# Dilated attention queries: one stored copy, laid out in rows of 128 per head by ScalarE, and projection blocks finished one at a time

## The chip, the cores and the metric

The kernel runs on one NeuronCore of a Trainium2 chip, as one program. The metric is device time in microseconds (us) of one execution, taken as the median of several. Engines are named as in the profile: PE (TensorE, matmuls), PEld (its weight loads, of the stationary operand), DVE (VectorE), ACT (ScalarE), POOL (GpSimd), SP (SyncE, which here only issues transfers). A letter q behind a name (SPq, ACTq, POOLq) is the engine's instruction queue when it issues a transfer. All matmul operands are float32 numbers, split into a rounded high part and the rest, so that one product is made of two or three matmuls.

## The reference

One decoder layer on 1024 tokens of width 1024. What matters here is the attention branch: 12 heads of 64 columns, three configurations with a softmax over each, weighted by their log-sum-exp. The kernel computes the third (dilation 16) inside the second (dilation 4): on 1024 tokens all that it reaches lies a multiple of four away, and a table of offsets counts twice what both reach. So it has two configurations, 0 and 1.

```python
C_HEADS = 12; HEAD_DIM = 64
C_CONFIGS = ((128, 1), (512, 4), (2048, 16))     # (window, dilation)

def _mixer_c(q, k, v, rel_table):
    q = q.reshape(bsz, s, C_HEADS, HEAD_DIM) * (HEAD_DIM ** -0.5)
    for window, dil in C_CONFIGS:
        o, l = _dilated_attn(q, k, v, window, dil, rel_table)   # blocks of 128 tokens, own and previous block
        outs.append(o); lses.append(l)
    wts = jax.nn.softmax(jnp.stack(lses, axis=0), axis=0)
    o = jnp.einsum('nbsh,nbshe->bshe', wts, jnp.stack(outs, axis=0))

z = xn @ w_in          # au, av, bx, bg, cq, ck, cv, z: all projections of the normed input
merged = gate_a * (out_a @ p_a) + gate_b * (out_b @ p_b) + gate_c * (out_c @ p_c)
x = x + g1 * (merged @ w_out)      # then the gated MLP, a second residual, a final norm
```

With dilation 4 a block holds every fourth token: queries 512j+r, 512j+r+4, and so on (a set r of four, j of two halves).

## The kernel before, in words

The program is one long run of matmuls on PE with all else arranged around it. It goes through these stages, in time of the profile: the norm and the first projections (0 to 192 us), the stream of projections (192 to 785 us), the attention (785 to 1190 us), the output projection, the gated MLP and the end (1190 to 1981 us).

**The stream.** A unit projects two blocks of 128 columns for all tokens in seven products (`ORDER`: A11, A12, S1, S2, S3, A22, S4), one in each slot, each of 12 matmuls. Results are evacuated into one tile `ot` (two buffers) that holds both blocks, m0 and m1. The first block m0 is complete with S4, the seventh slot, the second m1 with A22, the sixth. S3 adds into the PSUM bank that S2 has filled, so PE may start S3 only when ScalarE has evacuated S2 (line 165). S4 adds into bank z, which must first be read by line 269 on DVE, after line 267 on ACT. Behind the last slot of a unit `post` handles the two blocks: an activation over each (line 677) and a store to DRAM (678), or, for the queries and keys, `split_heads`, a generator that is put on the list `side` and of which one step is taken in each slot.

**Queries and keys.** `split_heads` makes the high part h of a block (ACT, line 924) and the low part in place (DVE, 927 or 929). For queries each of the two is also copied into an order in which the tokens of a block of 128 are sorted by their remainder r by 4 (ACT, line 933), and all four versions go to DRAM (918): sorted high and low, plain high and low. Keys are stored in two versions.

**Attention.** For a head `load_head` loads all four versions of q (1024 KB, line 1063, by POOL's queue) and k with both parts doubled (1065), and the bias table by SP's queue. `logits` (1197) makes one PSUM bank in each of seven slots. Slots 0 to 3 are configuration 0: the sorted queries `qp`, 128 columns that lie next to each other, are the stationary operand, 128 or 256 keys the moving one. Slots 4 to 6 are configuration 1: the stationary operand is `qn[:, 512*j+r : 512*j+r+509 : 4]`, the moving one `kt[:, r : r+4n-3 : 4]`, both with a step of four numbers. Slots 4 and 5 have four matmuls with 128 moving columns and then two with 256, slot 6 has four with 256. DVE adds the bias and takes the maximum (1219), ACT the exponential (1222), POOL works out the factors (`factors`, 1225), DVE scales and PE transposes (`turn`, 1249), PE multiplies with the values (`outputs`, 1265).

**Order.** In the stream the order on all five engines is written by hand (`Stream`). In the attention only PE's is: each step of a head h has a place in head units (load at h - 0.55, logits at h + 0.08 s, and so on), and between them lie steps of the `filler` (lines 1125 to 1159), the branch outputs times p_a, p_b, p_c (tile `gp`). The order on ACT, DVE, POOL and SP is set by a scheduler, so an edit in one place can shift rows in others. An engine works its queue in order: what waits holds all behind it.

**The seam** at 785 us: the last unit of the stream still runs while the first logits and the filler's first operands (`oT`, loaded by SP in line 1117 and split by ACT in line 116 and DVE or POOL in 117) come in, on the same ACT and DVE queues.

Of the kernel before, what the change touches and what calls it, by code (L numbers as in the profile page):

```python
# [36 lines left out]
LEAD, DQ, TM, DP, DO = 0.55, 0.08, 1.05, 0.11, 0.18  # L37
# [32 lines left out]
def trunk(ctx: ExitStack, tc: tile.TileContext, I: dict, out: bass.AP, dbg=None):  # L70
# [22 lines left out]
    def rows_scr(name, n):  # L93
# [3 lines left out]
    qk_scr = {n: [dram.tile(sh, F32, name=f"{n}{h}_scr") for h in range(NH)]  # L97
              for n, sh in (("q", [2, 2, HD, S]), ("k", [2, HD, S]))}
# [174 lines left out]
    def stream_ws(gb, tcomb, views, ot, post):  # L273
# [10 lines left out]
        for i, (wn, tn, bk) in enumerate(ORDER):  # L284
# [631 lines left out]
    def store_heads(name, ix, j, t):  # L916
        for i in range(2):
            nc.scalar.dma_start(qk_scr[name][2 * j + i][ix], t[HD * i:HD * i + HD, :])

    def split_heads(name, j, m, scale, hlp):  # L920

        mf = m.rearrange("p a b -> p (a b)")
        h = hlp().tile([P, S], F32R, tag="hl", bufs=3, name="hl")
        act.activation(h, mf, AF.Copy, scale=scale)
        yield
        if scale == 1.0:
            dve.tensor_tensor(mf.bitcast(F32R), mf, h.bitcast(F32), op=OP.subtract)
        else:
            dve.scalar_tensor_tensor(mf.bitcast(F32R), mf, scale, h.bitcast(F32), op0=OP.mult, op1=OP.subtract)
        for c, src in enumerate((h.bitcast(F32), mf)):  # L930
            if name == "q":
                dst = hlp().tile([P, S], F32, tag="hl", bufs=3, name="hlp")
# [5 lines left out]
            else:  # L938
                yield
# [787 lines left out]
```

## Time and profile before

| | us |
|---|---|
| median of 3 runs (lowest, highest) | 1984.4 (1983.62, 1989.04) |
| the profiled execution | 1982.27 |
| its span, first to last instruction | 1980.6 |
| PE, busy in the span | 1874.4 |
| DVE, busy in the span | 1287.9 |
| ACT, busy in the span | 899.5 |
| POOL, busy in the span | 633.8 |

The profile is read from PE: where PE has no idle time, work that other engines save costs or gives nothing, and only what PE itself issues counts. Where PE idles, the row names what ended the wait. Starts of matmuls that follow each other give the rate at which PE gets through them, which the durations in the rows don't, since matmuls overlap.

### The profile page before, as it was taken

How to read it: one execution, taken by the hardware profiler on the slowest of the kernel's cores; microseconds unless marked ns; L12 is line 12 of the kernel's file. 1: busy time of each engine (PE TensorE's matmuls, PEld its weight loads, DVE VectorE, ACT ScalarE, POOL GpSimd, SP SyncE). 2: the span in 40 equal slices, each digit the busy share in tenths (PEclk: the TensorE clock that was granted, in tenths of full speed). 3: DMA queues.
4: the chain of work that ended last, by engine and by line, in shares of the span. 5: the costliest groups of instructions: out<-in, count | busy, mean ns of one | idle time of the engine just before them, and what ended most of it. 6: DMA issues, size and time to landing. Idle time of an engine off the chain costs nothing.

```text
span 1980.6 us, 26351 instructions
## 1 busy us (share of the span) xinstructions
PE 1874.4 (95%) x9119; PEld 1508.4 (76%) x9119; DVE 1287.9 (65%) x2259; ACT 899.5 (45%) x1644; POOL 633.8 (32%) x1067
## 2 busy tenths in 40 slices
PE   6899999999999899899899999999999999999996
PEld 5767898877767677677777777877787887877885
DVE  6766576666666675555555765569767666557786
ACT  5344556664335633534434533444433443344543
POOL 6310000003111111244555565456544444300002
PEclk9899999999999999899999999999999999999998
DMA  9232435435556888777677445413334333477674
GB/s 326 70 122 84 140 104 165 140 129 173 172 178 218 291 243 235 217 167 188 166 167 186 126 169 181 150 64 123 122 114 149 99 97 124 135 271 254 201 228 147
DMA packets 248118, 328.61 MB, mean 166 GB/s; under 512 B 16551, under 2 KB 167315, under 8 KB 247984
## 3 DMA queue, kind: packets, MB, share of 16 engines
q1 hardware_dynamic: 197664, 184.07, 31.4%
q10 hardware_dynamic: 33744, 87.18, 12.1%
q0 software_dynamic: 16576, 55.67, 10.1%
q8 instruction: 72, 1.18, 0.2%
q14 instruction: 62, 0.51, 0.1%
HBM read 238.64 MB, written 88.22 MB: 165 GB/s over the span
## 4 chain that ended last, share of the span: by engine, by line
PE 72%; DMA 9%; DVE 6%; issue 6%; POOL 3%; ACT 2%; SPq 1%; ACTq 0%; DVEq 0%; POOLq 0%
PE g L191 18%; PE g L295 18%; PE gp L1152 7%; PE g L334 6%; PE g L1615 6%; PE go L1407 4%; PE sl L1214 3%; DMA adaw<-in_w_ada_dram 2%; PE g L215 2%; PE tp L1258 1%; PE o L1287 1%; PE gp L1370 1%; PE m L788 1%; DMA res<-x_scr 1%; PE o L1290 1%
## 5 line engine op out<-in xcount | busy, mean ns | idle before, releaser
L295 PE MATMUL g<-xs,wh 128*128 128x512 f32 x1344 | 435.9, 405 | 31.1 <-ACT ot L165 21.7
L191 PE MATMUL g<-xs,wh 128*128 128x512 f32 x1176 | 367.6, 394 | 9.5 <-DVE up L168 2.7
L295 PEld LDWEIGHTS g<-xs,wh 128*128 128x128 f32 x1344 | 251.3, 190 | 107.8 <-ACT ot L165 32.1
L116 ACT ACTIVATE wh<-raw 128x512 fp32r<-128x512 f32 (+2 forms) x251 | 147.2, 601 | 274.2 <-issue 58.8
L191 PEld LDWEIGHTS g<-xs,wh 128*128 128x128 f32 x1176 | 220.3, 188 | 63.0 <-ACT xs L116 3.1
L295 PE MATMUL g<-xs,wl 128*128 128x512 f32 x672 | 267.9, 399 | 0.0
L191 PE MATMUL g<-xs,wl 128*128 128x512 f32 x588 | 230.4, 393 | 0.0
L117 DVE TENSOR_TENSOR wl<-raw,wh 128x512 fp32r<-128x512 f32 (+2 forms) x180 | 129.8, 727 | 84.2 <-ACT wh L116 84.0
L1152 PE MATMUL gp<-oT,wh 128*128 128x512 f32 x512 | 171.7, 415 | 4.4 <-ACT oT L116 1.9
L295 PEld LDWEIGHTS g<-xs,wl 128*128 128x128 f32 x672 | 127.8, 190 | 31.2
L117 POOL TENSOR_TENSOR wl<-st,wh 128x512 fp32r<-128x512 f32 x63 | 104.0, 1651 | 144.3 <-ACT wh L116 139.4
L117 POOL TENSOR_TENSOR wl<-raw,wh 128x512 fp32r<-128x512 f32 (+2 forms) x71 | 92.3, 1301 | 123.1 <-ACT wh L116 108.4
L254 ACT ACTIVATE wh<-st 128x512 fp32r<-128x512 f32 x120 | 75.2, 627 | 120.6 <-DVE st L252 120.4
L191 PEld LDWEIGHTS g<-xs,wl 128*128 128x128 f32 x588 | 110.5, 188 | 24.9
L334 PE MATMUL g<-wh,xs 128*128 128x256 f32 x672 | 124.8, 286 | 0.0
L116 ACT ACTIVATE wh<-st 128x512 fp32r<-128x512 f32 x95 | 59.3, 628 | 138.9 <-PE g L191 96.8
L1222 ACT ACTIVATE pm<-pm,stat 128x128 f32<-128x128 f32 (+1 forms) x192 | 89.0, 465 | 58.0 <-DVE stat L1219 57.9
L1152 PEld LDWEIGHTS gp<-oT,wh 128*128 128x128 f32 x512 | 89.8, 192 | 27.2 <-issue 7.7
L334 PEld LDWEIGHTS g<-wh,xs 128*128 128x128 f32 x672 | 103.7, 188 | 1.6 <-issue 1.0
L1615 PE MATMUL g<-wl,wh 128*128 128x512 f32 x264 | 103.5, 392 | 0.0
L1615 PE MATMUL g<-wh,wl 128*128 128x512 f32 x264 | 103.4, 392 | 0.0
L1152 PE MATMUL gp<-oT,wl 128*128 128x512 f32 x256 | 102.7, 401 | 0.0
(321 smaller groups left out, 3790.2 us busy)
## 6 DMA issues: line engine op xcount, KB each, us to landing
raw<-in_w_in_dram SPq DMA_DIRECT2D x66, 512.0 KB, 5.7
raw<-in_f_wdown_dram SPq DMA_DIRECT2D x77, 256.0 KB, 3.7
adaw<-in_w_ada_dram SPq DMA_DIRECT2D x48, 256.0 KB, 5.4
g_scr<-ot ACTq DMA_DIRECT2D x24, 512.0 KB, 5.2
adaw<-in_w_ada_dram POOLq DMA_DIRECT2D x48, 256.0 KB, 5.1
raw<-g_scr SPq DMA_DIRECT2D x24, 512.0 KB, 3.6
qk<-q_scr POOLq DMA_DIRECT2D x12, 1024.0 KB, 6.1
qk<-k_scr POOLq DMA_DIRECT2D x24, 512.0 KB, 9.6
```

The source lines that it names most:

```text
L116: act.activation(h, src, AF.Copy)
L117: l_eng.tensor_tensor(l, src, h.bitcast(F32), op=OP.subtract)
L191: pe.matmul(banks[bk], a[:, k, :], b, start=(fresh and j == 0), stop=(j == 11), skip_group_check=True)
L215: pe.matmul(banks[i, h], a[:, k, :], b, start=(fresh and j == 0), stop=(not fresh and j == 11), skip_group_check=True)
L254: act.activation(it["h"], bl[name], AF.Copy)
L295: pe.matmul(banks[bk], a[:, k, :], b, start=(fresh and j == 0), stop=(j == 11), skip_group_check=True)
L334: pe.matmul(banks[t2][bk][:, 256 * i:256 * i + 256], a[:, sl], b[:, k % 2, :], start=(fresh and i == 0 and j == 0), stop=(j == 11), skip_g ...
L1152: pe.matmul(pt, a_[:, k % g, :], b_, start=(j == 0), stop=(j == 3 * n - 1))
L1214: pe.matmul(sb[:, of:of + n], lq, kt[:, ks], start=(of == 0 and kt is kh), stop=(kt is kl), skip_group_check=True)
L1222: act.activation(pm[:, of:of + n], pm[:, of:of + n], AF.Exp, scale=-1.0, bias=stt[:, cfg, 0, idx:idx + 1], accum_out=stt[:, cfg, 1, idx:id ...
L1407: pe.matmul(pt, a_[:, sl], b_, start=(k == 0 and j == 0), stop=(k == KD - 1 and j == 2))
L1615: pe.matmul(bank, a_[:, sl], b_, start=(start and j == 0), stop=(j == 2), skip_group_check=True)
```

## The change

Queries are stored in one version only, sorted, in two parts (high and low). The high part is written sorted in the one pass of ACT, the low part by four DVE instructions of 256 columns, and both parts of queries and keys have tiles of their own (`hl`), so that `ot` isn't written any more. `load_head` loads 512 KB of q. For configuration 1 a new step `turn_queries` copies the loaded sorted queries with two ACT instructions of 128x512 into a tile `qd`, in which the 128 queries of a set stand next to each other; slots 4 to 6 take their stationary operand from there, with a step of one. The keys keep their step of four. The load of a head moves from h - 0.55 to h - 1.2 (0.3 h for the first), `turn_queries` stands at h - 0.3, for head 0 at the end of the stream. In every unit of the stream the block m1 is finished by itself after A22, and m0 after S4.

```diff
-LEAD, DQ, TM, DP, DO = 0.55, 0.08, 1.05, 0.11, 0.18
+LEAD, DQ, TM, DP, DO = 1.2, 0.08, 1.05, 0.11, 0.18
@@ stream_ws
-                return later + (post(m0, m1) if wn == "S4" else [])
+                return later + (post(0, m0) if wn == "S4" else post(1, m1) if wn == "A22" else [])
@@ project
-        def post(m0, m1):
-            flat = [m.rearrange("p a b -> p (a b)") for m in (m0, m1)]
-            res = [(1, lambda i=i: act.activation(flat[i], flat[i], f)) for i in (1, 0) if f]
-            return res + [(2 if f else 1, lambda i=i: nc.scalar.dma_start(dst[j + i], flat[i])) for i in (1, 0)]
+        def post(i, m):
+            flat = m.rearrange("p a b -> p (a b)")
+            return [(1, lambda: act.activation(flat, flat, f)), (2, lambda: nc.scalar.dma_start(dst[j + i], flat))]
@@ split_heads
-        h = hlp().tile([P, S], F32R, tag="hl", bufs=3, name="hl")
-        act.activation(h, mf, AF.Copy, scale=scale)
+        h, l = [hlp().tile([P, S], F32R, tag="hl", bufs=3, name="hl") for _ in range(2)]
+        if name == "q":
+            by4 = [t.rearrange("p (t r i) -> p t r i", t=NT, r=4) for t in (h, l)]
+            src = mf.rearrange("p (t i r) -> p t r i", t=NT, r=4)
+            act.activation(by4[0], src, AF.Copy, scale=-0.125)
+            yield
+            for r in range(4):
+                dve.scalar_tensor_tensor(by4[1][:, :, r, :], src[:, :, r, :], -0.125, by4[0][:, :, r, :].bitcast(F32),
+                                         op0=OP.mult, op1=OP.subtract)
+        else:
+            act.activation(h, mf, AF.Copy)
+            yield
+            dve.tensor_tensor(l, mf, h.bitcast(F32), op=OP.subtract)
+        store_heads(name, 0, j, h.bitcast(F32))
         yield
-        if scale == 1.0:
-            dve.tensor_tensor(mf.bitcast(F32R), mf, h.bitcast(F32), op=OP.subtract)
-        else:
-            dve.scalar_tensor_tensor(mf.bitcast(F32R), mf, scale, h.bitcast(F32), op0=OP.mult, op1=OP.subtract)
-        for c, src in enumerate((h.bitcast(F32), mf)):
-            if name == "q":
-                dst = hlp().tile([P, S], F32, tag="hl", bufs=3, name="hlp")
-                act.activation(dst.rearrange("p (t r i) -> p t r i", t=NT, r=4),
-                               src.rearrange("p (t i r) -> p t r i", t=NT, r=4), AF.Copy)
-                store_heads("q", (1, c), j, src)
-                yield
-                store_heads("q", (0, c), j, dst)
...
+        store_heads(name, 1, j, l.bitcast(F32))
@@ load_head, and new
-        nc.gpsimd.dma_start(qq, qk_scr["q"][h].rearrange("a c b s -> (c b) a s"))
+        nc.gpsimd.dma_start(qp, qk_scr["q"][h].rearrange("c b s -> (c b) s"))
+    def turn_queries(qp):
+        qd = heads["hd"].tile([P, S], F32R, tag="qd", bufs=1, name="qd")
+        for j in range(0, S, HALF):
+            act.activation(qd[:, j:j + HALF].rearrange("p (r c i) -> p r c i", r=4, c=4),
+                           qp[:, j:j + HALF].bitcast(F32).rearrange("p (c r i) -> p r c i", r=4, c=4), AF.Copy)
+        return qd
@@ logits
-                    lq = qn[:, 512 * j + r:512 * j + r + 509:4]
+                    lq = st_["qd"][:, P * idx:P * idx + P]
@@ head_steps
-        yield h - LEAD, load
+        yield max(h - LEAD, 0.3 * h), load
+        if h:
+            yield h - 0.3, turn_heads
```

What this does to the queues is shown at three places. The first is ACT in the stream, in a unit of queries (`ot<-g` are the evacuations of lines 161, 165 and 267, `wh` the high parts of the next weights, `hl` and `hlp` the split queries, `q_scr` their store). Before, from the first slot's evacuation to line 165:

```order
L161 ACTIVATE ot<-g 128x512
L254 ACTIVATE wh<-st 128x512
L924 ACTIVATE hl<-ot 128x1024
L254 ACTIVATE wh<-raw 128x512
L933 ACTIVATE hlp<-hl 128x1024
L918 DMA q_scr<-hl 64x1024 x2
L254 ACTIVATE wh<-raw 128x512
L918 DMA q_scr<-hlp 64x1024 x2
L933 ACTIVATE hlp<-ot 128x1024
L918 DMA q_scr<-ot 64x1024 x2
L165 ACTIVATE ot<-g 128x512
```

and in the changed kernel, over the same slots:

```order
L926 ACTIVATE hl<-ot 128x1024
L161 ACTIVATE ot<-g 128x512
L254 ACTIVATE wh<-st 128x512
L917 DMA q_scr<-hl 64x1024 x2
L254 ACTIVATE wh<-raw 128x512
L917 DMA q_scr<-hl 64x1024 x2
L926 ACTIVATE hl<-ot 128x1024
L254 ACTIVATE wh<-raw 128x512
L917 DMA q_scr<-hl 64x1024 x2
L165 ACTIVATE ot<-g 128x512
```

Of the passes over 1024 columns only the 926 of block m0 stands between lines 161 and 165 now, with a weight split and two stores behind it; the copy 933 that stood directly ahead of line 165 is gone.

The second place is ACT at the seam (numbered tiles: `ot_6831` is the last unit's result, `oT_...` the filler's operands, `wh` with 128x384 the filler's weights, `pm` the first logits). Before:

```order
L165 ACTIVATE ot_6831<-g_6816 128x512
L116 ACTIVATE oT_7003<-oT_7004 128x512
L116 ACTIVATE wh_7280<-raw_7278 128x384
L116 ACTIVATE oT_6978<-oT_6979 128x512
L116 ACTIVATE wh_7284<-raw_7278 128x384
L267 ACTIVATE ot_6831<-g_6816 128x512
L1222 ACT_TABLE_LOAD
```

and in the changed kernel (`ot_6814` is the last unit's result there):

```order
L165 ACTIVATE ot_6814<-g_6799 128x512
L116 ACTIVATE oT_6987<-oT_6988 128x512
L116 ACTIVATE oT_6962<-oT_6963 128x512
L267 ACTIVATE ot_6814<-g_6799 128x512
L116 ACTIVATE wh_7283<-raw_7281 128x384
L116 ACTIVATE wh_7287<-raw_7281 128x384
L1230 ACT_TABLE_LOAD
```

Line 267 comes ahead of the two weight splits. In SP's queue the load of the `oT` that is split just ahead of line 267 also comes ahead of the load of those weights, and not behind it. Further on, ACT has `qd` of head 0 between the last unit's sigmoid and the exponentials of slot 2:

```order
L677 ACTIVATE ot_6814<-ot_6814 128x1024
L116 ACTIVATE oT_6977<-oT_6978 128x512
L116 ACTIVATE oT_7007<-oT_7008 128x512
L677 DMA g22_scr_139<-ot_6814 128x1024
L1076 ACTIVATE qd_6910<-qp_6781 128x512 x2
L1230 ACT_TABLE_LOAD
L1230 ACTIVATE pm_7058,stat_7017<-pm_7058,stat_7017 128x256 x2
L116 ACTIVATE oT_6982<-oT_6983 128x512
```

The third place is POOL in the attention, around the loads of one head (`sw`, `ex`, `dd`, `fc` are the factors, `wl` a low part of the filler's weights, `v` the values). Before:

```order
L1247 COPY fc<-ex 32x2 x16
L117 TENSOR_TENSOR wl<-raw,wh 128x384
L1171 COPY v_7695<-stat 1x1
L1175 COPY v_7698<-stat 1x1
L1230 COPY sw<-stat 32x4 x8
L1063 DMA qk<-q_scr 128x2x1024
L1065 DMA qk<-k_scr 64x2x1024 x2
```

and in the changed kernel:

```order
L1255 COPY fc<-ex 32x2 x16
L117 TENSOR_TENSOR wl<-raw,wh 128x384
L1057 DMA qp<-q_scr 128x1024
L1174 COPY v_7701<-stat 1x1
L1178 COPY v_7704<-stat 1x1
L1238 COPY sw<-stat 32x4 x8
L1059 DMA qk<-k_scr 64x2x1024 x2
```

The load of q stands earlier, ahead of the next head's first factor copies; the load of k stays where it was.

## Rows read from the trace of the kernel before

**Rows 1.** Busy us by stage: length, PE, PEld, DVE, ACT, POOL, granted clock, DMA share, GB/s.

```profile
620.00:700.00 80.00, 73.41 (x307) 56.42 (x305) 54.51 (x81) 49.64 (x53) 14.10 (x27) 0.98 0.87 286
785.00:825.00 40.00, 28.78 (x107) 21.94 (x106) 17.27 (x51) 22.64 (x53) 7.76 (x19) 0.83 0.80 240
825.00:1190.00 365.00, 357.33 (x2113) 283.35 (x2112) 213.41 (x717) 154.81 (x495) 199.95 (x574) 0.99 0.67 169
```

**Rows 2.** The same view, three stretches at the lower granted clock.

```profile
653.70:657.00 3.30, 3.15 (x7) 2.48 (x8) 1.88 (x4) 1.67 (x3) 1.03 (x2) 0.50 1.02 394
797.00:803.70 6.70, 4.71 (x11) 3.75 (x12) 3.32 (x8) 6.64 (x14) 1.07 (x1) 0.50 0.54 176
950.60:957.30 6.70, 5.00 (x18) 3.98 (x19) 4.53 (x17) 4.35 (x14) 3.13 (x3) 0.50 0.55 187
```

**Rows 3.** Timeline of PE, query units (start, length, operation, count [idle before, what ended it]).

```profile
629.67 0.72 PE L295 MATMUL g<-xs,wh 128*128 128x512 f32 x2 [0.69 <-ACT ot L165]
...
653.85 1.22 PE L295 MATMUL g<-xs,wh 128*128 128x512 f32 x2 [3.08 <-ACT ot L165]
...
679.16 0.73 PE L295 MATMUL g<-xs,wh 128*128 128x512 f32 x2 [2.81 <-ACT ot L165]
```

**Rows 4.** Timeline of ACT ahead of the second of these waits.

```profile
651.28 2.03 ACT L933 ACTIVATE hlp<-ot 128x1024 f32<-128x1024 f32 x1 [0.73 <-DVE adaa L975]
```

**Rows 5.** Timeline of PE at the seam, three of its waits.

```profile
788.47 0.73 PE L295 MATMUL g<-xs,wh 128*128 128x512 f32 x2 [2.19 <-ACT ot L165]
...
798.99 1.22 PE L295 MATMUL g<-xs,wh 128*128 128x512 f32 x2 [4.64 <-DVE ot L269]
...
812.98 0.50 PE L1152 MATMUL gp<-oT,wh 128*128 128x512 f32 x1 [0.56 <-ACT oT L116]
```

**Rows 6.** Timeline of ACT at the seam.

```profile
792.89 0.53 ACT L116 ACTIVATE wh<-raw 128x384 fp32r<-128x384 f32 x1 [3.31 <-DMA raw<-in_p_a_dram]
796.29 0.63 ACT L116 ACTIVATE oT<-oT 128x512 fp32r<-128x512 f32 x1 [2.88 <-DMA oT<-oa_scr]
...
797.24 0.58 ACT L267 ACTIVATE ot<-g 128x512 f32<-128x512 f32 x1
797.84 1.28 ACT L1222 ACT_TABLE_LOAD   x1
```

**Rows 7.** Timeline of PE, logits with a step of four, stretches of single matmuls.

```profile
1016.64 0.42 PE L1214 MATMUL sl<-qk 128*128 128x128 f32 x1
...
1016.88 0.54 PE L1214 MATMUL sl<-qk 128*128 128x256 f32 x1
...
1017.23 0.42 PE L1214 MATMUL sl<-qk 128*128 128x256 f32 x1
...
1022.67 0.42 PE L1214 MATMUL sl<-qk 128*128 128x256 f32 x1
...
1022.90 0.42 PE L1214 MATMUL sl<-qk 128*128 128x256 f32 x1
```

**Rows 8.** The same, logits with a step of one (two of 128, two of 256 columns).

```profile
1006.63 0.62 PE L1214 MATMUL sl<-qk 128*128 128x128 f32 x4
...
1006.80 0.45 PE L1214 MATMUL sl<-qk 128*128 128x256 f32 x2
...
1006.97 0.28 PE L1214 MATMUL sl<-qk 128*128 128x256 f32 x1
1007.09 0.39 PE L1152 MATMUL gp<-oT,wh 128*128 128x512 f32 x1
```

**Rows 9.** Weight loads by form, step four, then step one (count, busy us, mean ns).

```profile
L1214 PEld LDWEIGHTS sl<-qk 128*128 128x128 f32 x4 | 1.0, 328 | 0.2 <-issue 0.2
...
L1214 PEld LDWEIGHTS sl<-qk 128*128 128x128 f32 x4 | 0.5, 190 | 0.0
```

**Rows 10.** Timelines of POOL and PE around the longest wait inside the attention.

```profile
944.69 1.30 POOL L117 TENSOR_TENSOR oT<-oT 128x512 fp32r<-128x512 f32 x1 [5.11 <-ACT oT L116]
...
952.30 1.12 PE L1287 MATMUL o<-st,v 128*64 128x128 f32 x6 [4.44 <-DVE st L1263]
```

More of the change, by code (lines that the diff above doesn't have):

```diff
@@ L96, in trunk @@
     z_scr = {n: rows_scr(n, KW) for n in ("au", "bx", "bg")}
-    qk_scr = {n: [dram.tile(sh, F32, name=f"{n}{h}_scr") for h in range(NH)]
-              for n, sh in (("q", [2, 2, HD, S]), ("k", [2, HD, S]))}
+    qk_scr = {n: [dram.tile([2, HD, S], F32, name=f"{n}{h}_scr") for h in range(NH)]
+              for n in "qk"}
     g_scr = rows_scr("g", 3 * KD)
@@ L942, in project_heads @@
-    def project_heads(name, j, hlp):
-        def post(m0, m1):
-            def queue():
-                for i, m in ((1, m1), (0, m0)):
-                    side.append(split_heads(name, j + i, m, -0.125 if name == "q" else 1.0, hlp))
-            return [(1, queue)]
+        h, l = [hlp().tile([P, S], F32R, tag="hl", bufs=3, name="hl") for _ in range(2)]
[11 more added lines that the diff above has]
+            dve.tensor_tensor(l, mf, h.bitcast(F32), op=OP.subtract)
@@ L950, in project_heads, with post @@
+        store_heads(name, 0, j, h.bitcast(F32))
+        yield
+        store_heads(name, 1, j, l.bitcast(F32))
+    def project_heads(name, j, hlp):
+        def post(i, m):
+            return [(1, lambda: side.append(split_heads(name, j + i, m, hlp)))]
         return stream_ws(gb1, tcomb, pair_views(COL["c" + name], j), ot2, post)
@@ L1057, in load_head @@
     def load_head(h):
-        def tl():
-            return heads["hd"].tile([P, 2, S], F32R, tag="qk", bufs=2, name="qk") if h % 2 == 0 else \
-                wk.tile([P, 2, S], F32R, tag="ot", bufs=2, name="qk")
-        qq, kk = tl(), tl()
-        nc.gpsimd.dma_start(qq, qk_scr["q"][h].rearrange("a c b s -> (c b) a s"))
+        if h % 2 == 0:
+            qp = heads["hd"].tile([P, S], F32R, tag="qp", bufs=1, name="qp")
+            kk = heads["hd"].tile([P, 2, S], F32R, tag="qk", bufs=1, name="qk")
+        else:
+            qp, kk = [wk.tile([P, 2, S], F32R, tag="ot", bufs=2, name="qk") for _ in range(2)]
+            qp = qp[:, 0]
+        nc.gpsimd.dma_start(qp, qk_scr["q"][h].rearrange("c b s -> (c b) s"))
         for i in range(2):
             nc.gpsimd.dma_start(kk[HD * i:HD * i + HD], qk_scr["k"][h].rearrange("c b s -> b c s"))
-        qp, qn, kh, kl = qq[:, 0], qq[:, 1], kk[:, 0], kk[:, 1]
+        kh, kl = kk[:, 0], kk[:, 1]
         bt = heads["hd"].tile([P, 2, 256], F32, tag="bt", bufs=2, name="bt")
@@ L1075, in load_head @@
                 nc.sync.dma_start(bt[32 * q:32 * q + 32, cfg, :], src)
-        return qp, qn, kh, kl, bt
+        return qp, kh, kl, bt
+    def turn_queries(qp):
[4 more added lines that the diff above has]
+        return qd
     phase(["hd"], queue_heads)
@@ L1080, in trunk @@
     stream.call(marks)
+    heads["qd"] = turn_queries(heads[0][0])
     head0 = heads[0]
@@ L1191, in load, with turn_heads @@
             st_["in"] = load_head(h) if h else head0
+            if h == 0:
+                st_["qd"] = heads["qd"]
             st_["s"] = ap.tile([P, 2, 2, 8], F32, tag="stat", bufs=2, name="stat")
+        def turn_heads():
+            st_["qd"] = turn_queries(st_["in"][0])
         def values():
@@ L1197, in logits @@
         def logits(s_):
-            qp, qn, kh, kl, bt = st_["in"]
+            qp, kh, kl, bt = st_["in"]
             stt = st_["s"]
```

9 lines of the change are left out of this document (3 added, 6 removed).

## The prediction

> **What bounds the kernel now.** I read the busy time of each engine by stage first, then PE's waits inside a stage, then the starts of single matmuls. PE is the busiest engine in each of the stages that the change touches [rows 1]. So a gain must be PE idle time that goes, work that PE itself does faster, or a stretch at the lower clock that isn't entered. The stages differ. In the query units (620 to 700 us) PE idles 6.6 of 80 us, at the seam (785 to 825) 11.2 of 40, in the attention proper (825 to 1190) only 7.7 of 365 [rows 1]. In the first two a wait is the subject; in the third only what PE issues counts, as ACT (154.8 us), POOL (200.0) and DVE (213.4) have room in 365 us [rows 1]. From 1190 us on the change alters nothing but a few rows of the scheduler's order, which I cost at nothing.
>
> All sums are made against the profiled execution, 1982.3 us. It is 2.1 us below the median of 1984.4, so I take the gain off the median at the end.
>
> **Query units.** PE waits ahead of S3 for ACT's evacuation of S2: 0.69 us in the ordinary case, but 3.08 and 2.81 us in two of the three query units [rows 3]. The reader sees why in ACT's rows: the copy of line 933 runs from 651.28 for 2.03 us, line 165 can start only behind it, near 653.3, and PE goes on at 653.85 [rows 3, 4]. Each query block now has one strided pass on ACT in place of one plain and two strided ones, and none of it stands directly ahead of line 165. What is left between: block m0's pass, which I take to be as long as the strided copy, 2.03 us [rows 4], a split of weights and two store issues. A slot of 12 matmuls takes some 3.0 us (from 653.85 to 679.16 [rows 3], less the wait of 2.81 and 1.6 for the half clock below, in seven slots), and m0's pass is queued in the third slot, so it should be over before S2, in the fourth, ends. Both waits then fall to 0.69: 3.08 + 2.81 - 1.38 = 4.5 us. The first of them is also followed by 3.3 us at half clock, 1.2 GHz, with PE busy for 3.15 [rows 2]; at full clock that work takes half, 1.6 us less. Gain 6.1; if one of the waits stays, 3.
>
> The four DVE instructions replace one of the same 1024 columns. Even at twice its length DVE has cover, 54.5 of 80 us busy [rows 1], and what queues behind them are weight splits made four slots ahead. The extra function-table loads on ACT (1.28 us each [rows 6], three more by the order, where two sigmoids or gelus no longer stand together) lie in slots where line 165 isn't due; nothing for them. If a table load did fall ahead of an evacuation, it would cost its 1.28 us; this is inside the margin. Finishing m1 a slot sooner frees `ot` earlier, for which PE doesn't wait: nothing.
>
> **The seam.** PE's longest wait is 4.64 us ahead of S4, for line 269, which needs line 267 [rows 5]. ACT started 267 at 797.24 because the split ahead of it waited until 792.89 for weights and the next one until 796.29 for an `oT` load [rows 6]. S3 began at 788.47 [rows 5] and its 12 matmuls end near 791.5. In the new order neither the weights nor a late `oT` stands ahead of 267 (SP issues that `oT` load before the weights'), so 267 runs at some 791.6, DVE follows, and S4, two slots behind S3, starts without a wait near 794.5. That is 4.6 us, and up to 4.71 / 2 = 2.4 more if the half-clock stretch from 797 [rows 2] isn't entered.
>
> What is late next: the filler's operands. ACT's chain from the table load at 797.84 [rows 6] to the split that PE awaited at 812.98 [rows 5] takes 15.1 us, nearly all of it work on ACT. In the new kernel the table load comes after the two weight splits, whose data landed at 792.89, so near 793.9, 4 us sooner. Two `qd` passes are inserted, by ACT's nearest 128x512 row 0.63 each [rows 6], and a pair of exponentials and two splits move behind. So PE gets those operands some 4 us earlier, not 7. I take 4, with ends 0 (the chain eats it) and 7 (both parts of the wait's price).
>
> **The logits with dilation 4.** Here PE's own work changes, 12 heads with 16 such matmuls each, 8 of 128 and 8 of 256 moving columns. With a step of four one load takes 328 ns, with a step of one 190 [rows 9]. What counts is the spacing of starts. Step four: 1016.64 to 1016.88, 0.235 us, ahead of a 256; 1022.67 to 1022.90, 0.235 as well, for 256 columns [rows 7]. Step one: two of 128 and two of 256 take 0.46 together, 0.115 each, and the last 256 takes 0.12 [rows 8]. If only the load were slow, all 16 would gain 0.12.
>
> But the keys keep their step of four, and one row tells that they are slow too. With step four, the start that follows the first 256 comes 0.35 later, 1016.88 to 1017.23 [rows 7]; 0.235 is the load, so 0.115 is what 256 columns take beyond 128. With step one the same place has 1006.80 to 1006.97, 0.17 [rows 8], 0.05 beyond 0.115. 128 more columns cost twice as much with the step: streaming is at half rate as well, some 0.117 for 128 and 0.235 for 256. Then a 256 stays at 0.235 whatever its load does, and only the 128s gain, 8 x (0.235 - 0.117) = 0.94 us a head. The first load of a slot is 0.138 longer with the step [rows 9] and not hidden where short matmuls stand ahead, in about two slots of three: 0.2 a head. Together 1.1 x 12 = 13 us. Ends: 2 (only the first loads count) and 25 (all 16 gain 0.12, and the first loads). I take 13, since the 0.35 is measured in this very operation. The Trainium skill (SBUF — State Buffer, section "Door 1: The DMA port swizzle") says that reads which go to a new 16-byte line each time lose bandwidth; four float32 are 16 bytes, and it makes no difference between queries and keys, which speaks against the full 25. The two rows agree.
>
> **Its price on other engines.** Two ACT passes a head, 12 x 2 x 0.63 = 15 us, or twice that, of work on an engine with 210 us of room in this stage [rows 1]. In ACT's order they stand mostly ahead of slot 6's exponentials of the head before and must wait for that slot's logits on PE, 0.08 head away; the exponentials behind would wait for the same logits. The rows are due at slot 4, half a head later. Nothing. The transfers shrink from 1024 to 512 KB a head, with DMA at 0.67 [rows 1]: nothing. POOL gets the q load earlier in its queue; behind it stand factor copies and weight splits. The tile that it fills was given free at logits that PE has finished by then: nothing. The wait of 4.44 us at 952.30 comes from a split on POOL that waited 5.11 us with the factor copies behind it [rows 10]; that order hardly changes and the wait stays.
>
> **Sum.** 6 + 4 + 13 = 23 us: 1959 for the profiled execution, 1961 as a median.
>
> **Rivals.**
> 1. *The loads alone are slow.* The logits gain 25, the sum is 35: 1949 us. For it: 328 against 190 ns is plain [rows 9]. Against it: the 0.35 [rows 7]. The same time would follow if loads did not run beside matmuls at all: 192 x 0.138 = 26 us. Against that stands a spacing of 0.235 that is shorter than the load's 328 [rows 7, 9]. The Trainium skill (TensorE: Matmul & The Clock Gate, section "The mechanism") lets loads overlap running matmuls only when they use other row groups; the trace doesn't agree. Chance 0.14.
> 2. *The attention gives it back.* PE gets ahead, and the filler's operands, already late at the seam, or POOL's chain become the limit; the logits' gain shrinks to 2: 6 + 4 + 2 = 12, 1972 us. For it: the schedule is not re-timed to PE, and POOL is busy 200 of 365 us in long chains [rows 1, 10]. Against it: PE waits just 7.7 us there now. Chance 0.18.
> 3. *Slower: the earlier load of q holds POOL.* If at that place its tile isn't free, POOL stands with factor copies and weight splits behind it, as at 944.69. One such hold costs what that one does: 4.44 us of wait, and 5.00 / 2 = 2.5 of work at half clock behind it [rows 2, 10], 7 us. Three holds leave a gain of 2; from the fourth head on the kernel is slower, 1961 + 28 = 1989, at eight of twelve heads 2017. For it: one tile for `qp` and `qd` each, where q and k had two buffers. Against it: by the order the freeing logits stand more than half a head ahead. Chance 0.06.
> 4. *It does what it says, and it doesn't matter:* waits only move and the half-clock stretches come elsewhere; 1980 to 1984. Chance 0.04.
>
> **How the numbers follow.** Forecast 0.58, the rivals 0.14, 0.18, 0.06, 0.04. The range takes the ends of the three terms: 6 + 7 + 25 = 38 gives 1946, 3 + 0 + 2 = 5 gives 1979; I cut the upper end to 1977, since all three low ends at once are unlikely. This leaves out rivals 3 and 4 and part of 2. Within 0.3% (6 us, about what a measurement of this kernel can tell from no change): 0.06, rival 4 and a bit of 2. Faster 0.88, slower 0.06.
>
> **What would show it.** PE's waits ahead of S3 in the query units at 0.7 and no half clock there; no wait ahead of the last S4 and the seam shorter by about 4; in slots 4 and 5 starts 0.12 apart for 128 columns, in slot 6 still 0.235. If slot 6 runs at 0.12, rival 1 holds. If new waits for `oT`, `wl` or the factors appear in the attention, rival 2 or 3. A wait of logits for `qd` would prove the cover wrong.

## The result, and the profile after

The changed kernel takes 1956.8 us (median of 4 runs, 1955.37 to 1959.26) against 1984.9 (4 runs of the kernel before beside it): a ratio of 0.986, 95% interval 0.984 to 0.988. The forecast was 1961 with a range from 1946 to 1977; the time fell by 28 us where 23 had been forecast. The profiled execution took 1959.3, the slowest of the four; its span is 1957.6 against 1980.6, so 23.0 less, as the sum said. That it comes out to the microsecond is luck: 26.8 were gained up to the last logits, and 3.8 lost behind them. This table is read from the starts of PE's rows in the two profiles. The profiled execution of before was 2.6 us faster than the median beside it, that of the change 2.5 slower; this is why the median fell by 5 us more than the profile.

| PE starts (us) | before | after | after less before | forecast |
|---|---|---|---|---|
| first logits | 785.2 | 780.9 | -4.3 (3.8 of it in the query units) | -6 |
| first `gp` | 806.0 | 795.4 | -10.6, so -6.3 at the seam | -4 |
| last logits | 1137.5 | 1110.7 | -26.8, so -16.2 in the attention | -13 |
| end of the span | 1980.6 | 1957.6 | -23.0, so +3.8 behind it | 0 |

The busy time of PE over the whole span in the profile after (share, instructions), and then the same view of stretches as [rows 1]; the seam now lies some 5 to 10 us earlier, so its stretch does too.

```profile
PE 1863.1 (95%) x9119; PEld 1493.1 (76%) x9119; DVE 1290.8 (66%) x2277; ACT 899.3 (46%) x1659; POOL 636.3 (33%) x1067
```

```profile
620.00:700.00 80.00, 75.63 (x320) 57.54 (x319) 64.92 (x108) 33.76 (x44) 15.50 (x29) 1.00 0.71 232
780.00:820.00 40.00, 34.26 (x151) 27.56 (x150) 22.98 (x73) 25.36 (x60) 13.53 (x50) 0.91 0.97 250
825.00:1190.00 365.00, 360.75 (x2168) 279.75 (x2168) 218.07 (x707) 172.02 (x522) 209.97 (x555) 0.99 0.59 159
```

In the query units ACT has 33.8 us of work in 80 where it had 49.6, the DMA share is 0.71 for 0.87, and the clock is whole. All waits ahead of S3 there are the ordinary 0.69, the answer to [rows 3] (timeline of PE after):

```profile
630.05 0.74 PE L295 MATMUL g<-xs,wh 128*128 128x512 f32 x2 [0.69 <-ACT ot L165]
...
652.79 0.74 PE L295 MATMUL g<-xs,wh 128*128 128x512 f32 x2 [0.69 <-ACT ot L165]
...
674.71 0.72 PE L295 MATMUL g<-xs,wh 128*128 128x512 f32 x2 [0.69 <-ACT ot L165]
```

Two waits for DVE are new in the query units. The low part of the queries now takes 2.2 us on DVE where it took 1.22, and before it starts it waits until an earlier store has landed, since it writes into one of the three `hl` tiles. Line 252 stands behind it on DVE, and ACT's next weight split, two store issues, line 267 and DVE's line 269 follow late (rows of DVE, then of PE):

```profile
629.99 2.19 DVE L929 SCALAR_TENSOR_TENSOR hl<-ot,hl 128x256 fp32r<-128x256 f32 x4 [3.44 <-DMA q_scr<-hl]
```

```profile
637.80 0.50 PE L295 MATMUL g<-xs,wh 128*128 128x512 f32 x1 [0.71 <-DVE ot L269]
...
681.51 0.74 PE L295 MATMUL g<-xs,wh 128*128 128x512 f32 x2 [0.92 <-DVE ot L269]
```

At the seam PE waits 1.05 where it waited 2.19, has no wait ahead of S4 any more, and then 3.67 for the bank of S4's result, where it had waited 1.75 (rows of PE, then of ACT, the answer to [rows 5, 6]):

```profile
783.00 0.73 PE L295 MATMUL g<-xs,wh 128*128 128x512 f32 x2 [1.05 <-ACT ot L165]
...
795.37 1.19 PE L1155 MATMUL gp<-oT,wh 128*128 128x512 f32 x2 [3.67 <-DVE ot L172]
```

```profile
786.11 0.60 ACT L267 ACTIVATE ot<-g 128x512 f32<-128x512 f32 x1 [1.26 <-PE g L295]
788.11 0.94 ACT L116 ACTIVATE wh<-raw 128x384 fp32r<-128x384 f32 x2 [1.40 <-DMA raw<-in_p_a_dram]
789.07 1.28 ACT L1230 ACT_TABLE_LOAD   x1
```

Line 267 runs as soon as PE has delivered its bank, and the weights land behind it. In slots 4 and 5 the starts of 128 columns now lie 0.11 to 0.12 apart; the two 256s of such a slot lie 0.23 apart, where it was 0.35; those of 256 in slot 6 are still at 0.23 (timeline of PE; a row begins at the first matmul of a merged piece, and the rows shown are neighbours ahead of the dots and behind them). A load lasts 196 ns for 328 [rows 7, 9]:

```profile
1021.69 0.67 PE L1222 MATMUL sl<-qk,qd 128*128 128x128 f32 x3
1021.80 0.78 PE L1222 MATMUL sl<-qk,qd 128*128 128x128 f32 x3
1021.92 0.66 PE L1222 MATMUL sl<-qk,qd 128*128 128x256 f32 x2
1022.15 0.43 PE L1222 MATMUL sl<-qk,qd 128*128 128x256 f32 x1
...
1028.38 0.64 PE L1222 MATMUL sl<-qk,qd 128*128 128x256 f32 x2
1028.61 0.65 PE L1222 MATMUL sl<-qk,qd 128*128 128x256 f32 x2
```

```profile
L1222 PEld LDWEIGHTS sl<-qk,qd 128*128 128x128 f32 x16 | 2.3, 196 | 0.1
```

**What was given back behind the attention.** After 1190 us the order of PE's work is the same, but this execution has half-clock stretches at 1196.8, 1329.9, 1374.3 and 1749.8, 20.4 us long in all, where the profiled execution of before has two of 3.4, at 1223.6 and 1776.6 (both have two more in the last 50 us, of much the same length). Three of the four (the columns are those of [rows 1]):

```profile
1329.90:1336.70 6.80, 6.18 (x15) 4.82 (x16) 6.70 (x8) 4.98 (x9) 5.02 (x4) 0.50 0.25 80
1374.30:1377.70 3.40, 3.40 (x9) 2.65 (x8) 2.79 (x4) 1.29 (x3) 1.00 (x2) 0.50 0.26 106
1749.80:1756.50 6.70, 4.27 (x10) 3.40 (x11) 3.97 (x6) 4.29 (x8) 0.00 (x0) 0.50 1.04 395
```

PE is busy for 13.85 us in these three, work of 6.9 at full clock by an estimate from the two clocks. The stretch from the last logits to the end took 846.9 here, 843.1 before, and 840.6 to 847.4 in the profiles of the experiments. So 3.8 lies within the scatter of single executions, and the other three runs (1955.4, 1955.5, 1958.2) fit that. A small part may be lasting: the six profiles of kernels that start from the changed one (itself among them) have a mean of 845.3 there, the six others 843.4. What starts those stretches was not tried.

### The profile page after: what moved, and what is told of

Its sections match the earlier page's. It is cut to its first block, busy times and chain, and to the rows that moved or that the text cites. A ratio compares the mean times of both kernels' runs of the same rounds, so it can differ in the third digit from the quotient of the medians.

```text
span 1957.6 us, 26362 instructions
## 1 busy us (share of the span) xinstructions
PE 1863.1 (95%) x9119; PEld 1493.1 (76%) x9119; DVE 1290.8 (66%) x2277; ACT 899.3 (46%) x1659; POOL 636.3 (33%) x1067
## 4 chain that ended last, share of the span: by engine, by line
PE 75%; DMA 8%; DVE 7%; issue 4%; ACT 3%; POOL 3%; SPq 0%; DVEq 0%; ACTq 0%; POOLq 0%
PE g L295 21%; PE g L191 18%; PE gp L1155 6%; PE g L334 6%; PE g L1625 6%; PE go L1417 4%; PE sl L1222 3%; PE g L215 2%; PE tp L1266 1%; PE o L1295 1%; PE gp L1380 1%; PE m L787 1%; PE o L1298 1%; DMA res<-x_scr 1%; DMA raw<-in_p_a_dram 1%
## 5 line engine op out<-in xcount | busy, mean ns | idle before, releaser
L117 DVE TENSOR_TENSOR wl<-raw,wh 128x512 fp32r<-128x512 f32 (+2 forms) x180 | 126.5, 709 | 90.4 <-ACT wh L116 90.2
L1155 PEld LDWEIGHTS gp<-oT,wh 128*128 128x128 f32 x512 | 90.4, 193 | 27.7 <-issue 7.7
```

The source lines that it names most:

```text
L117: l_eng.tensor_tensor(l, src, h.bitcast(F32), op=OP.subtract)
L1155: pe.matmul(pt, a_[:, k % g, :], b_, start=(j == 0), stop=(j == 3 * n - 1))
```

## The experiments

Times are medians beside runs of the kernel before on the same chip; where a ratio is given it is to those runs. The stage lengths below are from the profiles: query units from the S3 ahead of them (608.9 in before) to the S3 behind them (700.7), seam from the first logits to the first `gp`, attention from there to the last logits. Each length is that of one execution.

| us | query units | seam | attention | whole, ratio (interval) |
|---|---|---|---|---|
| before | 91.8 | 20.8 | 331.5 | 1 |
| after | 88.0 | 14.5 | 315.3 | 0.986 (0.984 to 0.988) |
| e1, queries at step one | 90.4 | 20.1 | 322.2 | 0.995 (0.993 to 0.997) |
| e2, queries and keys | 91.7 | 21.4 | 313.8 | 0.990 (0.988 to 0.992) |
| e3, after, keys too | 88.1 | 14.6 | 315.0 | 0.984 (0.982 to 0.985) |
| e4, copies half as long | 92.7 | 20.5 | 333.1 | 1.000 (0.999 to 1.001) |
| e5, before, blocks one by one | 107.9 | 14.1 | 333.5 | 1.003 (1.001 to 1.004) |
| e6, after, blocks together | 90.4 | 17.4 | 314.9 | 0.987 (0.985 to 0.990) |
| e7, after, late loads | 87.7 | 14.6 | 313.0 | 0.983 (0.981 to 0.985) |
| e8, before, half the stores | 86.4 | 21.0 | 339.9 | 1.001 (1.000 to 1.003) |
| e9, after, stores doubled | 120.9 | 14.8 | 313.0 | 1.001 (1.000 to 1.003) |
| e10, after, q load in two | 87.6 | 15.3 | 314.9 | 0.985 (0.983 to 0.988) |

**e1, e2 and e3: the step of queries and of keys.**

```diff
 e1: before
-                    lq = qn[:, 512 * j + r:512 * j + r + 509:4]
+                    lq = qn[:, P * idx:P * idx + P]
 e2: e1, and                       e3: after, and
-                    ks = slice(r, r + 4 * n - 3, 4)
+                    ks = slice(0, n)
```

> The kernel before with one edit: slots 4 to 6 take as stationary operand 128 queries that lie next to each other in the plain copy, so other queries than the reference's (configuration 1 is computed with the wrong queries); loads, stores, splits and keys stay as they were. Theory (queries and keys both slow with a step of four, the keys still have it): starts 0.118 apart for 128 columns, 0.235 still for 256; per head 2 x 0.54 + 0.14 = 1.2 us, 14 us in all, near 1970. Rival 1 (only the load is slow): 256 columns at 0.12 as well, 25 us, near 1960. Rival 2 (given back to other engines): under 4 us. The waits of 3.1 and 2.8 us in the query units and of 4.6 us at the seam stay by all of them.

> As the run before, and the keys of slots 4 to 6 are also read next to each other (configuration 1 is computed with the wrong queries and keys). Theory: the 256s go from 0.235 to 0.12, 8 x 0.115 = 0.9 us a head more, 11 us beyond the run before, near 1960; the 128s stay at 0.115. Rival 1: no change against the run before.

> The changed kernel with the keys of slots 4 to 6 read next to each other (configuration 1 is computed with the wrong keys). Theory: slot 6 goes from 0.233 to 0.118 a matmul, 11 us less than the changed kernel, near 1946, if PE still sets the pace of the attention. If other engines set it by now: under 4 us, with new waits of PE for DVE, ACT or POOL.

Medians: e1 1974.3 and e2 1968.1 beside 1986.8, e3 1954.0. The stretch called attention can be divided, from start to start of PE's rows, into the time that PE spends on each kind of matmul and the waits over 0.15 us:

| us | before | e1 | e2 | after | e3 |
|---|---|---|---|---|---|
| logits, slots 4 and 5 | 37.4 | 24.8 | 19.1 | 25.0 | 19.6 |
| logits, slots of four 256s (slot 6 and others) | 32.6 | 31.8 | 27.0 | 31.9 | 27.1 |
| all other matmuls | 252.4 | 254.7 | 254.4 | 252.9 | 254.9 |
| waits of PE | 9.0 | 11.0 | 13.4 | 5.6 | 13.4 |

The step of the queries alone gives 13.5 us of logits in e1 and 13.2 in the changed kernel (the first two rows, before rounding): the term as forecast, and not 25. The keys' step is worth another 10.5 of logits in e2, so the keys with a step of four are slow by themselves. In slot 6 a 256 then takes 0.119 for 0.233 (medians), as with a step of one [rows 8]. One such slot, from its first matmul to the row behind it, takes 1.00 us in e1 and 0.58 in e2 (rows of PE of e1, then of e2):

```profile
1014.96 1.18 PE L1214 MATMUL sl<-qk 128*128 128x256 f32 x4
1015.96 0.51 PE L1258 MATMUL tp<-ident,pm 128*128 128x128 f32 x3
```

```profile
1013.68 0.74 PE L1214 MATMUL sl<-qk 128*128 128x256 f32 x4
1014.26 0.60 PE L1258 MATMUL tp<-ident,pm 128*128 128x128 f32 x4
```

That settles the rival of the loads. The whole of e2 is only 6.2 faster than e1, where 11 were expected. For e1 turns 13.5 us into 9.3 (other matmuls 2.3 longer, waits 2.0 longer), in e2 the waits grow by another 2.4, and e3 gains 10.1 of logits on the changed kernel and loses nearly all of it again: 7.8 more waits and 2.0 on the other matmuls, some of which run at half clock behind such a wait. Two waits of PE in e3, where the changed kernel has 1.49 at the first place and none over 0.4 at the second:

```profile
824.66 0.58 PE L1222 MATMUL sl<-qk 128*128 128x256 f32 x1 [4.95 <-DVE stat L1227]
...
869.88 0.33 PE L1298 MATMUL o<-st,v 128*64 128x128 f32 x2 [3.20 <-ACT st L1269]
```

So e3's expected gain was not there: at such places PE has caught up with DVE's maxima and ACT's scaled rows. As a whole e3 can't be told from the changed kernel (ratios of 0.984 and 0.986, their intervals overlap). The rival that the attention gives the gain back is wrong for this change and right for the next step of the same kind.

The Trainium skill (SBUF — State Buffer, section "Door 1: The DMA port swizzle") says that each access which goes to a new 16-byte line pays a penalty, and doesn't set the operand that is loaded apart from the one that moves. Both pay here: a load takes 328 ns with a step of four numbers and 196 with one, a 256 in slot 6 takes 0.233 and 0.119 us.

**e4 and e8: what holds ACT in the query units.** e4 makes each copy of line 933 plain, 1.06 us for 2.03, and stores as much. e8 keeps every pass and stores only one of the two versions, from the copies.

```diff
 e4: before
-                act.activation(dst.rearrange("p (t r i) -> p t r i", t=NT, r=4),
-                               src.rearrange("p (t i r) -> p t r i", t=NT, r=4), AF.Copy)
+                act.activation(dst, src, AF.Copy)
 e8: before
-                store_heads("q", (1, c), j, src)
                 yield
                 store_heads("q", (0, c), j, dst)
@@ load_head
-        nc.gpsimd.dma_start(qq, qk_scr["q"][h].rearrange("a c b s -> (c b) a s"))
+        for i in range(2):
+            nc.gpsimd.dma_start(qq[:, i], qk_scr["q"][h][0].rearrange("c b s -> (c b) s"))
```

> The kernel before with the two sorted copies of a query block on ScalarE written in plain order, 1.05 in place of 2.05 us each (the sorted queries are then the plain ones, so configuration 0 is computed with the wrong order of queries). Everything else, stores and seam too, as before. Theory (the pass ahead of the evacuation of S2 is what PE waits for in the query units): waits of 3.08 and 2.81 us shrink by 1 to 2.1 us each, without the 3.4 us at half clock, 3 to 6 us in all; near 1980. Rival (the store issues on ScalarE's queue hold the evacuation): waits stay, no change.

> The kernel before, with only the copied (plain) version of the queries stored, high and low, and read for both uses: four stores of 64x1024 a block in place of eight, none of them from ot, while all passes of ACT stay, the 2-us copy of line 933 directly ahead of line 165 among them. Configuration 0 gets queries in another order, so the output is another. Theory (landings and issues of stores hold ACT's queue): the waits ahead of S3 in the query units fall from 3.08 and 2.81 to 0.7 to 1.2, first logits some 3 to 5 us earlier, the whole 1979 to 1983. Rival (the length of the passes of ACT): the waits stay at 2.5 or more, within 2 us of before.

(The text on record for e8 has the versions the wrong way round: the copies are the sorted ones, and it is configuration 1 that reads queries in another order.) In e4 the copies halve, the waits hardly fall (2.69 and 2.52 for 3.08 and 2.81), and the whole stays, 1987.5 beside 1986.8. The copy ahead of line 165 just starts later, with more idle time ahead of it (rows of ACT, and of PE behind them):

```profile
652.65 1.06 ACT L933 ACTIVATE hlp<-ot 128x1024 f32<-128x1024 f32 x1 [1.25 <-DVE adaa L974]
652.67 1.67 ACTq L918 DMA_DIRECT2D q_scr<-ot  x2
654.39 0.60 ACT L165 ACTIVATE ot<-g 128x512 f32<-128x512 f32 x1 [0.67 <-issue]
```

```profile
655.04 0.51 PE L295 MATMUL g<-xs,wh 128*128 128x512 f32 x1 [2.69 <-ACT ot L165]
```

In e8, with all copies at their full length, the waits are 0.99 and 1.12, and the query units are 5.4 us shorter, more than in the changed kernel:

```profile
654.53 0.50 PE L295 MATMUL g<-xs,wh 128*128 128x512 f32 x1 [0.99 <-ACT ot L165]
...
676.74 0.50 PE L295 MATMUL g<-xs,wh 128*128 128x512 f32 x1 [1.12 <-ACT ot L165]
```

So it was the stores. In the kernel before the row that I should have followed stands 8 us ahead of the wait: line 161 idles 3.01 until a store of `ot` has landed, and everything on ACT is late from there. Counted from the S3 of the unit ahead (629.67 before [rows 3], 632.45 in e8), line 161 starts at 15.81 before and at 13.44 in e8, line 165 at 23.55 and 21.44: the 2.4 that the landing costs arrive at line 165 nearly whole. The same happens ahead of the second wait, where line 161 starts at 670.75, just behind the landing of the next store of `ot` (670.64). e8 takes away two things at once, half of the stores and `ot` as a source of stores; e9 below takes up the second (rows of ACT of before; then busy time of that stretch, where the DMA share is 0.99, and of the same stretch after, 0.73):

```profile
645.48 0.60 ACT L161 ACTIVATE ot<-g 128x512 f32<-128x512 f32 x1 [3.01 <-DMA q_scr<-ot]
...
651.30 1.72 ACTq L918 DMA_DIRECT2D q_scr<-ot  x2
```

```profile
640.00:654.00 14.00, 10.91 (x47) 8.45 (x46) 9.86 (x15) 10.26 (x11) 2.27 (x5) 0.99 0.99 320
```

```profile
640.00:654.00 14.00, 13.31 (x57) 10.44 (x56) 10.91 (x20) 7.85 (x9) 2.15 (x4) 1.00 0.73 246
```

e8 as a whole is no faster, 1991.0 beside 1987.8, where 1979 to 1983 was expected: its attention is 8.4 us longer, nearly all of it lost at three places, near 946, 1038 and 1100. At the first two DVE holds a weight split of the filler that waits 4.30 and 6.95 us for its operand, with rows of the softmax behind it. At 1038 these are the reciprocal of the factors (1036.95) and the scaled rows behind it, for which PE then waits 3.16; in the kernel before the reciprocal (1031.45) is ahead of that split (1038.30) in DVE's queue. So at these places it is the scheduler's order on DVE. Why that order came out differently in e8 stays open; e10 below takes away one idea.

**e5 and e6: blocks one by one.** e5 puts this part of the change alone into the kernel before, e6 takes it out of the changed one.

```diff
 e5: before (post split in two, as in the change)
-                return later + (post(m0, m1) if wn == "S4" else [])
+                return later + (post(0, m0) if wn == "S4" else post(1, m1) if wn == "A22" else [])
 e6: after
-                return later + (post(0, m0) if wn == "S4" else post(1, m1) if wn == "A22" else [])
+                return later + (post(1, m1) + post(0, m0) if wn == "S4" else [])
```

> The kernel before, with one part of the change: a unit's block m1 is finished behind A22, m0 behind S4. Queries are stored and read as before. In ACT's order at the seam line 267 now stands ahead of the two weight splits, as in the changed kernel. Theory (finishing blocks one by one is what makes the seam shorter): no wait ahead of S4 at the seam, first logits to first gp some 6 us shorter, the whole 1979 to 1981. Rival (the seam got shorter because the query stores or the qd passes came out otherwise): the 4.64 us wait ahead of S4 stays and the whole is within 2 us of before. In the query units the stores are as many as before; theory: PE's waits ahead of S3 stay at 2.5 to 3.1 there; rival (the early start of the split spreads them): 0.7.

> The changed kernel, with one part undone: both blocks of a unit are finished behind S4 again. In ACT's order the 1024-column pass over a query block (some 2.0 us) stands directly ahead of line 165 again, and line 267 stands behind the weight splits at the seam. Theory: the waits ahead of S3 in the query units stay at 0.69, since the four stores fewer per block removed them, and the seam gets its wait ahead of S4 of 3 to 5 us back: 1961 to 1964. Rival 1 (a long pass directly ahead of line 165 is what PE waits for): waits of 2 to 3 us ahead of S3 as well, 1965 to 1968. Rival 2 (the order of finishing is worth nothing): within 2 us of the changed kernel, 1955 to 1959.

At the seam the theory holds, with both signs: e5 shortens it from 20.8 to 14.1, with no wait ahead of S4, and e6 brings the wait ahead of S4 back and makes it 17.4 (PE of e6; then line 267 on ACT, in e6 behind a weight split that waits for its load, in e5 as soon as PE has delivered):

```profile
794.03 0.79 PE L295 MATMUL g<-xs,wh 128*128 128x512 f32 x1 [3.24 <-DVE ot L269]
```

```profile
790.41 0.52 ACT L116 ACTIVATE wh<-raw 128x384 fp32r<-128x384 f32 x1 [4.34 <-DMA raw<-in_p_a_dram]
...
792.04 0.58 ACT L267 ACTIVATE ot<-g 128x512 f32<-128x512 f32 x1
```

```profile
805.98 0.60 ACT L267 ACTIVATE ot<-g 128x512 f32<-128x512 f32 x1 [1.75 <-PE g L295]
```

In the query units it missed. e5 doesn't leave PE's waits at 3 us, it makes them 6.84, 7.79 and 5.05, and the whole is 5.8 us slower (1993.6 beside 1987.8), where 1979 to 1981 was expected. Rows of ACT and PE of e5:

```profile
626.91 7.00 ACTq L917 DMA_DIRECT2D q_scr<-hlp  x2
634.01 1.06 ACT L923 ACTIVATE hl<-ot 128x1024 fp32r<-128x1024 f32 x1 [6.61 <-DMA raw<-in_w_in_dram]
634.97 0.58 ACT L165 ACTIVATE ot<-g 128x512 f32<-128x512 f32 x1
```

```profile
635.61 1.22 PE L295 MATMUL g<-xs,wh 128*128 128x512 f32 x2 [6.84 <-ACT ot L165]
```

Two issues of stores that take 1.1 us elsewhere take 7.0 here: ACT stands in its own issue. The releaser named in the next row, a weight load, is not what line 923 needs. In e6 the 2.06-us pass stands directly ahead of line 165 again, and PE waits 1.65, 1.80 and 1.79, between the 0.69 of the theory and the 2 to 3 of its rival: with the stores halved a pass at that place, which itself starts only after some 2.6 us of idle time on ACT, costs 1.0 to 1.1 us a unit beyond the ordinary 0.69, where the wait before was 2.1 to 2.4 beyond it. e6 in all: 1965.3 (five runs from 1958.2 to 1965.9), in the profiles 4.6 us behind the changed kernel at the last logits.

**e9: the stores doubled.** The counterpart of e8: the changed kernel, with none of its passes altered and no store from `ot`. It keeps the new order of finishing, in which e5 waits too.

```diff
+        if name == "q":
+            for i in range(2):
+                nc.scalar.dma_start(qk_scr["w"][2 * j + i][c], t[HD * i:HD * i + HD, :])
```

> The changed kernel, with each store of queries issued twice, the second time to another place in DRAM that nobody reads: eight stores of 64x1024 a block as before the change, all from hl tiles, none from ot; one pass of ACT a block as in the changed kernel. Theory (the number of stores, by the time they take to issue and land on ACT's queue): PE's waits ahead of S3 in the query units come back, 2.5 us or more in at least two of three, DMA share above 0.8 there, 620 to 700; the query units 4 to 16 us longer, the whole 1961 to 1973. Rival (what held ACT was that ot itself was a source of stores, so that line 161 and the passes waited for its landing): the waits stay at 0.69 to 1, the whole within 3 us of the changed kernel.

The waits are 10.80, 9.94 and 10.23, the query units 32.9 us longer (4 to 16 were expected), and the whole, 1987.8 beside 1984.3, loses all that the change had won. Rows of ACT, and the wait of PE behind them:

```profile
626.54 7.57 ACTq L920 DMA_DIRECT2D w_scr<-hl  x2
634.16 2.01 ACT L929 ACTIVATE hl<-ot 128x1024 fp32r<-128x1024 f32 x1 [9.80 <-DMA w_scr<-hl]
...
639.09 0.60 ACT L165 ACTIVATE ot<-g 128x512 f32<-128x512 f32 x1 [2.40 <-issue]
```

```profile
639.74 0.79 PE L295 MATMUL g<-xs,wh 128*128 128x512 f32 x1 [10.80 <-ACT ot L165]
```

Again an issue that lasts 7.57, and behind it a pass that waits for a landing before it may write its `hl` tile again (three buffers), and then 2.4 us of issues ahead of line 165. So twice the stores suffice in this order, and `ot` as their source isn't needed for it. Eight stores a block, none from `ot`, in the old order were not run, so how much of the 3.01 before is due to `ot` as the source stays open; so does whether the number of stores counts or their bytes, since both runs change the two together.

One part of what was expected fell: the DMA share is 0.68 from 620 to 700, not above 0.8. But that is a mean over a stage in which ACT stands still for long. While the long issues last, the DMA engines are nearly full (busy time in e9 from 626.50 to 634.00, then in e5 from 626.90 to 633.90: DMA share 0.91 and 0.87, last column GB/s):

```profile
626.50:634.00 7.50, 2.43 (x11) 1.62 (x9) 0.00 (x0) 0.00 (x0) 0.35 (x1) 0.93 0.91 350
```

```profile
626.90:633.90 7.00, 1.86 (x8) 1.15 (x7) 1.29 (x2) 0.50 (x1) 0.00 (x0) 0.87 0.87 337
```

So these runs do not part a hold of ACT's queue from a want of transfer rate at that moment.

**e7 and e10: the loads of a head.**

```diff
 e7: after
-        yield max(h - LEAD, 0.3 * h), load
+        yield h - LEAD, load              # LEAD 0.55 for 1.2
 e10: after
-        nc.gpsimd.dma_start(qp, qk_scr["q"][h].rearrange("c b s -> (c b) s"))
+        for i in range(2):
+            nc.gpsimd.dma_start(qp[HD * i:HD * i + HD], qk_scr["q"][h][i])
```

> The changed kernel with the load of a head back at h - 0.55 (it had moved to h - 1.2). Theory (the place of the load costs and gives nothing as long as the rows are due half a head later): within 3 us of the changed kernel, 1954 to 1960, with no wait of logits. Rival (the early load of q holds POOL with factor copies behind it): 1950 or less, with fewer waits of PE for stat, st and sl in the attention. Other rival (late loads make turn_queries late): 5 to 30 us slower, waits of logits for qd.

> The changed kernel with the load of q of a head in two transfers of 64x1024 in place of one of 128x1024, the same bytes: one issue more on POOL's queue per head, some 0.57 us each by the row of the changed kernel (one q issue 0.58). Theory (that second issue is what cost the kernel before with half the stores about 8 us between the first gp and the last logits): 5 to 9 us slower than the changed kernel, new waits of PE for pm, stat or st in the attention. Rival (that loss came from another order of POOL and DVE there, and an issue costs nothing): within 3 us of the changed kernel, 1954 to 1960.

e7 takes 1954.9, e10 1954.4, both within 3 us of the changed kernel, and no wait of logits for `qd` appears in e7. Against the runs of the kernel before beside them they gain 32.9 and 29.9, where the change gained 28.1; the intervals of the ratios overlap. (e10 has one wait of 4.56 us at 826.7, for `pm`, and its attention is no longer for it.) So neither the place of the load nor one issue more on POOL is shown to cost anything here, and in the changed kernel a second issue does not cost what e8's attention lost. The hold of POOL by the load, of the third rival, does occur in the changed kernel, once as long as 3.44 us, and no wait of PE over 0.4 us follows it; in e7, with the load later, it is there too (2.40 us at 936.02):

```profile
937.35 0.58 POOL L1057 DMA_DIRECT2D qk<-q_scr  x1 [3.44 <-PE sl L1222]
```

## Why the prediction was right, and where its steps were wrong

- **Logits, 13 forecast.** 13.2 measured by the division above, by the mechanism given: with the keys at a step of four the 128s go to 0.118 and the 256s of slot 6 stay at 0.233. e1 shows it for the queries' step alone, e2 that the keys' step is the other half. That the sum fits so closely is partly luck. The 128s and the first interval of slot 6 gave 10.7 us, less than the 1.1 a head of the forecast. Another 2.8 came from a 256 that the prediction held fixed ("a 256 stays at 0.235 whatever its load does"): the start behind the first 256 of slots 4 and 5 came 0.35 later before and comes 0.23 later now.
- **The attention as a whole, -16.2 against -13.** The failed step is "that order hardly changes and the wait stays". The 4.44 us ahead of 952.30 [rows 10] are gone; the longest wait inside is now 1.81, and the waits of the stretch fell from 9.0 to 5.6.
- **Query units, 6 forecast, 3.8 measured** (4.3 up to the first logits). The waits ahead of S3 went as forecast (3.08 and 2.81 to 0.69), the half clock at 653 went too, but it was worth 0.9, not 1.6 (PE's time outside the waits: 84.5 before, 83.6 after), and new waits of 0.71 and 0.92 for line 269 took 1.6 back. Here "even at twice its length DVE has cover" failed: the length came out as said, but DVE also waits for a landing ahead of it. The cause of the old waits was wrong too: the step "line 165 can start only behind it" took the instruction directly ahead of the late one for what delays it. Halving it (e4) gives 0.3 to 0.4 us a wait; halving the stores (e8) gives 1.7 to 2.1. Four stores fewer a block stand in no term of the prediction.
- **The seam, 4 forecast, 6.3 measured.** The mechanism was right (line 267 freed from the weights and the late `oT`). Of the 6.3, 3.9 are waits: 2.19, 4.64 and 1.75 became 1.05, nothing and 3.67. The other 2.4 are the same 44 matmuls, 12.2 us of PE before and 9.8 now: before, S4 ran at half clock [rows 2]. The half clock was entered all the same, from 794.0, but it now falls on the last wait and on the `gp` matmuls behind it, so its cost lies in the next stage and was not saved.
- **"Finishing m1 a slot sooner frees `ot` earlier, for which PE doesn't wait: nothing"** failed. Line 267's new place at the seam comes with that part of the change (e5, e6), 6.7 us in the kernel before and 2.9 in the changed one. With eight stores a block it costs 16 us in the query units (e5). So the new order of finishing relies on the smaller number of stores, and a sum by parts could not show it.
- **Behind the attention**, 0 forecast, 3.8 lost in the profiled execution by half-clock stretches. This hid in the profile that the terms up to there had been 3.8 short; the median gained 28.
- **Rivals.** Loads alone slow: refuted (e1, e2). The attention gives it back: not here, but at once in e3. POOL held by the load: the hold is there, and no cost of it is shown. That it doesn't matter: no.

## What to carry to other kernels

When an engine is late, follow its queue back to the first instruction that waited for something other than its own queue. The long pass directly ahead may only pass the delay on: here it was a store's landing 8 us earlier. Count the stores that an engine issues as work and as holds of its tiles, and look for fewer of them before you shorten its passes. Try a change of order together with what it relies on: the same reordering cost 16 us in one stage with eight stores a block, and with four it gained 2.4 there (e6 against the changed kernel).

## What the runs showed of the hardware that I had not expected

- A pair of store issues of 256 KB each on ACT's queue takes 1.1 us in the ordinary case, and 7.0 (e5) or 7.57 (e9) when many are under way, with the DMA engines 0.87 and 0.91 busy meanwhile. The ACT engine does next to nothing in that time (0.50 and 0.00 us of work in the two stretches). The mean share over the stage, 0.68 in e9, doesn't show it; the share of the stretch does.
- The same 256 moving columns in slot 6 go from 0.233 to 0.119 us when their step falls from four numbers to one (e1, e2); with a step of four they took 0.24 and 0.23 with a stationary operand at step four and at step one (before, after). Keys at step one beside queries at step four were not run.
